# Gate projections of the first branch: from single blocks of 128 columns to pairs of blocks with seven half-size products

## The chip, the cores and the metric

The kernel runs on one core of a Trainium2 chip. The metric is the device time of one execution in microseconds (us). Five engines work side by side, each on its own queue in order: TensorE (PE, matrix products; its weight loads are shown as PEld), VectorE (DVE), ScalarE (ACT), GpSimd (POOL) and SyncE (SP, which here only issues DMAs). Sixteen DMA engines move data for all queues.

## The reference, cut to what matters

One encoder layer on 512 tokens of width 1024, in float32:

```
h = rmsnorm(x, pre_mix_w)
proj = h @ w_in                                   # q, k, v of two branches, and two gates
g_a, g_b = sigmoid(proj[..., gates] + b_gate)     # 1024 columns each
y_a = diff_attention(...)                         # branch A, 512 wide
y_b = neighbourhood_attention_2d(...)             # branch B, 512 wide
merged = g_a * (y_a @ w_branch_a) + g_b * (y_b @ w_branch_b)
x = x + rmsnorm(merged @ w_out, post_mix_w)
h = rmsnorm(x, pre_ffn_w)
f = (silu(h @ w_gate) * (h @ w_up)) @ w_down
x = x + rmsnorm(f, post_ffn_w)
```

The change concerns g_a (the gate of the first branch) and the merge.

## The kernel before

**Precision.** Each float32 operand is split into a high and a low part of a shorter type: the high part is a copy by ScalarE, the low part the difference, formed by VectorE. A product A x B is three matrix instructions into one bank: high x high, high x low, low x high (`mm3`, lines 217 to 219). Splitting a weight unit of 128 x 1024 takes one ACTIVATE (line 147) and one subtraction (line 153). Where VectorE is short of time, the low part is formed in another way: ScalarE writes minus the high part (line 73) and GpSimd issues a DMA that adds the raw values to it (line 74).

**Weights.** The class `Weights` holds all weight units in the order of their use. `load_to` issues their DMAs on SP into a pool of five raw buffers, `split_to` splits them in order, and each unit has a `place`: the pool for its two parts. `w` has four large buffers (`place_w`), `up` has 18 slots of 4 KB per partition for activations and temporaries, `up2` has 11 such slots and exists from the end of attention on. A slot of a pool is taken when the first instruction that writes the tile is placed.

**Stages.** After the norm, the transposed tokens lie in `hT`, as high and low parts, for the whole mixer. An interleaved list of steps (`main`, four steps per weight unit) runs the projections of both branches, with the stages of attention put between them by a table of positions (`events`). The last steps of `main` are the eight gate blocks of the second branch (`gate_b`, line 858: 24 matrix instructions of 512 columns, a sigmoid, and one product with what the second branch had given, kept in `pbt`). The last attention event falls into the fifth of these blocks. Then comes the loop that the change rewrites, lines 892 to 912, once for each of eight blocks of 128 gate columns:

```python
        W.split_to(UG["a", m] + 3)
        for k in range(KD):        # KD = 8: 24 matrix instructions of 512 columns
            mm3(bank, ...)
        nc.scalar.activation(sig, bank, AF.Sigmoid, bias=bg[:, m:m + 1])
        for k in range(4):         # branch A's projection: 12 of 512 columns
            mm3(bk2, ...)
        nc.vector.tensor_mul(sig, sig, bk2)
        nc.vector.tensor_add(sig, sig, pbt[m // 2][:, m % 2])
```

followed by the split of the merged block into a tile `mg`. The output projection (line 1005 on, weight units `UO`) needs all eight `mg`, for each block of 128 tokens in turn.

**The form with seven products.** The feed-forward stage already computes pairs of column blocks by a Winograd form of Strassen's scheme (line 1101 on). The 1024 x 256 weights of a pair are cut into quarters A11, A12, A21, A22 (512 rows by 128 columns, seen transposed), the tokens into quarters B11, B12, B21, B22 (512 features by 256 tokens). Weight sums S1 to S4 (`pair_steps`, line 64: six steps s0 to s5, run while the pair before is multiplied) and token sums T1 = B12 - B11, T2 = B22 - T1, T3 = B22 - B12, T4 = B21 - T2 (`t_sums`, made once) give seven products of 12 matrix instructions with 256 columns, instead of eight; small VectorE additions put the results together. The tables `ORDER` and `ORDER0` name the order of the products; the last of both is A22 x T4.

**What sets the order.** A planner lays out each engine's queue ahead of time from the program order and estimated durations: an instruction is taken early where its engine would stand idle and its operands and slot are there. In the start of the kernel (`manual_schedule`) the order is as written.

Of the kernel before, what the change touches and what calls it, by code (L numbers as in the profile page):

```python
# [14 lines left out]
S = 512  # L15
# [162 lines left out]
def block_kernel(ctx: ExitStack, tc: tile.TileContext, x, pre_mix_w, w_in,  # L178
# [71 lines left out]
    def add_branch(nm, w, j):  # L250
        n = w.shape[1]
        src = dram(w, 256 * j, [[n, 128], [128 * n, 4], [1, 256]])
        UBR[nm, j] = W.add(src, (4, 256), place_w)
# [11 lines left out]
    for m in range(8):  # L265
        UG["a", m] = W.add(cols128(w_in, 3072 + 128 * m), (8, 128), place_w)
        if m % 2 == 0:
            add_branch("a", w_branch_a, m // 2)
# [266 lines left out]
    def feat_slot(unit, evac, start=None):  # L535
        st = {}

        def step(q):
            def go():
                if q == 0:  # L540
                    st["bank"] = pmm.tile([128, 512], F32, tag="mm", name="mm")
                if q == 1:
                    W.split_to(unit + 4)
# [40 lines left out]
    def pb_slots(j):  # L584
        for s2 in range(2):
# [3 lines left out]
            def step(q, m=m, s2=s2, st=st):  # L589
                def go():  # L590
                    if q == 0:
                        st["bank"] = pmm.tile([128, 512], F32, tag="mm", name="mm")
                        if s2 == 0:
                            W.split_to(UBR["b", j] + 4)
# [271 lines left out]
    for m in range(8):  # L866
        gate_b(m)
    last_ev = max(events)
    assert last_ev < len(main), (last_ev, len(main))
    for n in range(len(main)):  # L870
# [3 lines left out]
        if n == last_ev:  # L874
            atk.close()
            stk_ps.close()
            up2 = ctx.enter_context(tc.tile_pool(name="u2", bufs=11))

# [4 lines left out]
    def wo_pl():  # L883
        wo_cnt[0] += 1
        if wo_cnt[0] <= 5:
            return place_pool(up2)()
        return (up2.tile([128, 1024], F32R, tag="u", name="whi"),
                up.tile([128, 1024], F32R, tag="u", name="wlo"))

    wo_place.fn = wo_pl  # L890
    mg = []
    for m in range(8):
        bank = pmm.tile([128, 512], F32, tag="mm", name="mm")
        bk2 = psB.tile([128, 512], F32, tag="b", name="b")
        if m == 4:
            W.raw_bufs = 3
        W.split_to(UG["a", m] + 3)
        hi, lo = W.get(UG["a", m])
        for k in range(KD):
            mm3(bank, hi[:, k], lo[:, k], hT[k // 4][:, k % 4, 0], hT[k // 4][:, k % 4, 1], k == 0, k == KD - 1)  # L900
        sig = U(F32, [128, 512], "sig")
        nc.scalar.activation(sig, bank, AF.Sigmoid, bias=bg[:, m:m + 1])
        hi, lo = W.get(UBR["a", m // 2])
        cs = slice(128 * (m % 2), 128 * (m % 2) + 128)
        for k in range(4):
            mm3(bk2, hi[:, k, cs], lo[:, k, cs], ya[k][:, 0], ya[k][:, 1], k == 0, k == 3)
        nc.vector.tensor_mul(sig, sig, bk2)
        nc.vector.tensor_add(sig, sig, pbt[m // 2][:, m % 2])
        t = U(F32R, [128, 2, 512], "mg")
        nc.scalar.activation(t[:, 0], sig, AF.Copy)  # L910
        nc.vector.tensor_sub(t[:, 1], sig, t[:, 0].bitcast(F32))
        mg.append(t)
# [173 lines left out]
    for m in range(2):  # L1086
# [4 lines left out]


    ORDER = (("A11", "B11", "A", "p"), ("S2", "T2", "B", "v"), ("S1", "T1", "C", "v5"),
             ("S3", "T3", "D", "c22"), ("S4", "B22", "C", "c12"), ("A12", "B21", "A", "c11"),
             ("A22", "T4", "D", "c21"))

    ORDER0 = (("A11", "B11", "A", "p"), ("A12", "B21", "F", "p11"), ("S4", "B22", "E", ""),
              ("S2", "T2", "B", "v"), ("S1", "T1", "C", "v5 p12"), ("S3", "T3", "D", "c22"),
              ("A22", "T4", "D", "c21"))
    gu = {}  # L1100
    for n, unit in enumerate(pairs):
# [4 lines left out]
        bank = {}  # L1106
        G = U(F32, [128, 2, 512], "G")
        pv = U(F32, [128, 3, 256], "pv")
        for i, (sn, tn, c, ev) in enumerate(ORDER if n else ORDER0):
            opens = c not in bank  # L1110
            if opens:
                bank[c] = psB.tile([128, 512], F32, tag="b", name="b")[:, :256]
            (sh, sl), (th, tl) = parts[sn], TQ[tn]
            kw = {} if opens else {"skip_group_check": True}
            for k in range(4):
                nc.tensor.matmul(bank[c], sh[:, k], th[:, k], start=opens and k == 0,  # L1116
                                 stop=False, **kw)
                nc.tensor.matmul(bank[c], sh[:, k], tl[:, k], start=False, stop=False, **kw)  # L1118
                nc.tensor.matmul(bank[c], sl[:, k], th[:, k], start=False, stop=k == 3, **kw)  # L1119
            for what in ev.split():  # L1120
                if what == "p":
                    nc.scalar.activation(pv[:, 0], bank["A"], AF.Copy)
                elif what == "v":
                    nc.vector.tensor_add(pv[:, 1], pv[:, 0], bank["B"])  # L1124
                elif what == "v5":
                    nc.vector.tensor_add(pv[:, 2], pv[:, 1], bank["C"])  # L1126
                elif what == "c22":
                    nc.vector.tensor_add(G[:, 1, 256:], pv[:, 2], bank["D"])
                elif what == "c12":
                    nc.vector.tensor_add(G[:, 0, 256:], pv[:, 1], bank["C"])  # L1130
                elif what == "p12":
                    nc.vector.tensor_add(G[:, 0, 256:], pv[:, 2], bank["E"])
# [138 lines left out]
```

## Time and profile before

| | |
|---|---|
| median of 3 runs | 747.43 us (747.38 to 747.66) |
| the profiled execution | 746.6 us, span 744.8 us |
| PE busy | 729.5 us, 98% of the span |
| PEld / DVE / ACT / POOL busy | 86% / 65% / 51% / 11% |
| granted TensorE clock, mean | 0.996 |
| DMA moved | 101.49 MB |

The span goes from the first to the last instruction; the profiled execution's own time has 1.8 us more around it. Durations of matrix instructions in the trace overlap (they are pipelined); what a product costs is read from the distance between starts.

### The profile page before, as it was taken

Reading aid. Unit: us, or ns where it says so; the run is one execution under the profiler, and the core shown is the slowest. Engines: PE = TensorE matmul, PEld = TensorE weight load, DVE = VectorE, ACT = ScalarE, POOL = GpSimd, SP = SyncE. Lnnn points to the kernel's source line nnn. Section 1 sums busy time; section 2 is a strip of 40 time slices with the busy share of each in tenths; the row PEclk is TensorE's granted clock in tenths of the full one; section 3 lists DMA queues with packets and bytes.
Section 4 is the critical chain, followed back from the end, with each engine's and each line's share of the span. In section 5 each row is a group of like instructions: output and inputs, shape, how many; then the busy total and the mean of one; then the engine's idle time right before and its main releaser. Section 6 shows DMA issues by size and latency. Waiting matters only on the chain. (4 is left out here: it accounts for less than half of the span.)

```text
span 744.8 us, 11240 instructions
## 1 busy us (share of the span) xinstructions
PE 729.5 (98%) x4368; PEld 643.5 (86%) x4368; DVE 481.8 (65%) x841; ACT 376.3 (51%) x611; POOL 83.0 (11%) x129
## 2 busy tenths in 40 slices
PE   8999999999999999999999999999999999999996
PEld 7887888877888888887889999999999998888884
DVE  6625788888776633466457987777778879222333
ACT  6413665665666722463124866666666656212211
POOL 1010001122330000000011111111111110000000
PEclk9999999999999999999999999999999999999999
DMA  9537645333311223263714588878878872443112
GB/s 257 173 87 210 169 107 163 100 99 99 99 58 30 85 74 96 91 220 114 197 49 148 122 179 198 198 181 195 188 173 186 215 192 103 142 169 118 51 45 68
DMA packets 102582, 101.49 MB, mean 136 GB/s; under 512 B 3537, under 2 KB 85473, under 8 KB 102530
## 3 DMA queue, kind: packets, MB, share of 16 engines
q1 hardware_dynamic: 96080, 82.82, 38.4%
q0 software_dynamic: 6448, 17.97, 12.0%
q8 instruction: 34, 0.56, 0.3%
q14 instruction: 18, 0.15, 0.1%
q10 hardware_dynamic: 2, 0.00, 0.0%
HBM read 74.56 MB, written 4.19 MB: 106 GB/s over the span
## 5 line engine op out<-in xcount | busy, mean ns | idle before, releaser
L153 DVE TENSOR_TENSOR w<-raw,w 128x1024 fp32r<-128x1024 f32 x67 | 82.0, 1226 | 83.7 <-ACT w L147 82.7
L147 ACT ACTIVATE w<-raw 128x1024 fp32r<-128x1024 f32 x67 | 70.4, 1053 | 61.8 <-PE b L219 51.8
L217 PE MATMUL mm<-hT,w 128*128 128x512 f32 x256 | 100.9, 394 | 0.3 <-DVE v L393 0.3
L218 PE MATMUL mm<-hT,w 128*128 128x512 f32 x256 | 99.9, 390 | 0.0
L219 PE MATMUL mm<-hT,w 128*128 128x512 f32 x256 | 99.8, 390 | 0.0
L1118 PE MATMUL b<-Tl,w 128*128 128x256 f32 x240 | 66.8, 278 | 0.0
L1116 PE MATMUL b<-Th,w 128*128 128x256 f32 x240 | 66.8, 278 | 0.0
L1119 PE MATMUL b<-Th,w 128*128 128x256 f32 x240 | 66.8, 278 | 0.0
L217 PEld LDWEIGHTS mm<-hT,w 128*128 128x128 f32 x256 | 48.1, 188 | 10.3 <-DVE v L393 0.7
L219 PEld LDWEIGHTS mm<-hT,w 128*128 128x128 f32 x256 | 48.1, 188 | 10.3
L218 PEld LDWEIGHTS mm<-hT,w 128*128 128x128 f32 x256 | 48.1, 188 | 9.2
L217 PE MATMUL b<-w,fh 128*128 128x512 f32 x144 | 56.0, 389 | 0.0
L218 PE MATMUL b<-w,fh 128*128 128x512 f32 x144 | 56.0, 389 | 0.0
L219 PE MATMUL b<-w,fl 128*128 128x512 f32 x144 | 56.0, 389 | 0.0
L74 POOL DMA_DIRECT2D w<-raw x40 | 34.5, 864 | 168.9 <-ACT w L73 131.1
L1119 PE MATMUL b<-Q,w 128*128 128x256 f32 x160 | 44.5, 278 | 0.9 <-DMA w<-raw 0.8
L1119 PEld LDWEIGHTS b<-Th,w 128*128 128x128 f32 x240 | 45.4, 189 | 0.0
L1116 PEld LDWEIGHTS b<-Th,w 128*128 128x128 f32 x240 | 45.3, 189 | 0.0
L1118 PEld LDWEIGHTS b<-Tl,w 128*128 128x128 f32 x240 | 45.3, 189 | 0.0
L1118 PE MATMUL b<-Q,w 128*128 128x256 f32 x160 | 44.3, 277 | 0.0
L1116 PE MATMUL b<-Q,w 128*128 128x256 f32 x160 | 44.3, 277 | 0.0
L982 ACT ACTIVATE junk<-b 128x512 f32<-128x512 f32 x16 | 9.6, 598 | 61.6 <-PE b L219 56.8
(231 smaller groups left out, 1883.0 us busy)
## 6 DMA issues: line engine op xcount, KB each, us to landing
raw<-in_w_in_dram SPq DMA_DIRECT2D x40, 512.0 KB, 4.2
raw<-in_w_gate_dram SPq DMA_DIRECT2D x22, 512.0 KB, 4.4
raw<-in_w_up_dram SPq DMA_DIRECT2D x22, 512.0 KB, 5.0
raw<-in_w_down_dram SPq DMA_DIRECT2D x22, 512.0 KB, 3.2
w<-raw POOLq DMA_DIRECT2D x20, 512.0 KB, 5.8
K<-K SPq DMA_DIRECT2D x24, 256.0 KB, 3.0
w<-raw POOLq DMA_DIRECT2D x20, 256.0 KB, 5.2
x<-in_x_dram SPq DMA_DIRECT2D x8, 512.0 KB, 8.9
```

Of the source, the lines that this page charges most:

```text
L74: nc.gpsimd.dma_start(lo, src, accum_op=ALU.add)
L147: self.nc.scalar.activation(hi, raw, AF.Copy)
L153: (engine or self.nc.vector).tensor_sub(lo, raw, hi.bitcast(F32))
L217: nc.tensor.matmul(bank, sh, mh, start=first, stop=False)
L218: nc.tensor.matmul(bank, sh, ml, start=False, stop=False)
L219: nc.tensor.matmul(bank, sl, mh, start=False, stop=last)
L982: nc.scalar.activation(junk, bs, AF.Square, scale=1.0 / 32.0, accum_out=ss[:, n:n + 1])
L1116: nc.tensor.matmul(bank[c], sh[:, k], th[:, k], start=opens and k == 0, stop=False, **kw)
L1118: nc.tensor.matmul(bank[c], sh[:, k], tl[:, k], start=False, stop=False, **kw)
L1119: nc.tensor.matmul(bank[c], sl[:, k], th[:, k], start=False, stop=k == 3, **kw)
```

## The change

The eight gate blocks of the first branch become four pairs in the seven-product form. `pair_products` is the feed-forward stage's loop body, made a function and called from both places. The token sums for it are made from `hT` by `ga_ahead`: for each quarter, ScalarE copies the high part and a DMA of GpSimd adds the low part (`block`); the four sums are formed by VectorE in place over the quarters, and split (`total`; T3 and T4 with the DMA form of the low part). These steps, and the first pair's weight steps, are taken two at a time behind the last eleven steps of `main`, after the last attention event. The pair's branch weight (256 columns) is split once per pair, into `up2`, and its two branch products and merges follow the pair's seven products. Three of the large weight buffers are held by a pair (parts A11/A12, S2/S1, S3/S4), and A22 lies in `up`. Output weight 0 goes to `w`, 1 to `up`, 2 to 5 to `up2`.

```diff
--- before.py
+++ after.py
@@ -247,10 +247,10 @@
 
     UBR = {}
 
-    def add_branch(nm, w, j):
+    def add_branch(nm, w, j, place=place_w):
         n = w.shape[1]
         src = dram(w, 256 * j, [[n, 128], [128 * n, 4], [1, 256]])
-        UBR[nm, j] = W.add(src, (4, 256), place_w)
+        UBR[nm, j] = W.add(src, (4, 256), place)
 
     order = ([("qk", "b", i) for i in range(4)] + [("qk", "a", 0), ("qk", "a", 1),
              ("qk", "a", 2), ("pb", 0), ("qk", "a", 3), ("pb", 1), ("pb", 2), ("pb", 3)])
@@ -262,10 +262,14 @@
     UG = {}
     for m in range(8):
         UG["b", m] = W.add(cols128(w_in, 4096 + 128 * m), (8, 128), place_w)
-    for m in range(8):
-        UG["a", m] = W.add(cols128(w_in, 3072 + 128 * m), (8, 128), place_w)
-        if m % 2 == 0:
-            add_branch("a", w_branch_a, m // 2)
+    ga_place = Late1()
+    br_place = Late()
+    UGP = []
+    for p in range(4):
+        UGP.append(W.add_pair([cols128(w_in, 3072 + 128 * m) for m in (2 * p, 2 * p + 1)],
+                              (8, 128), ga_place))
+        for j in {1: (0,), 2: (1,), 3: (2, 3)}.get(p, ()):
+            add_branch("a", w_branch_a, j, br_place)
     wo_place = Late()
     UO = {}
     for k in range(KD):
@@ -540,7 +544,7 @@
                 if q == 0:
                     st["bank"] = pmm.tile([128, 512], F32, tag="mm", name="mm")
                 if q == 1:
-                    W.split_to(unit + 4)
+                    W.split_to(min(unit + 4, UGP[0]))
                 hi, lo = W.get(unit)
                 for k in (2 * q, 2 * q + 1):
                     mm3(st["bank"], hi[:, k], lo[:, k], hT[k // 4][:, k % 4, 0], hT[k // 4][:, k % 4, 1],
@@ -591,7 +595,7 @@
                     if q == 0:
                         st["bank"] = pmm.tile([128, 512], F32, tag="mm", name="mm")
                         if s2 == 0:
-                            W.split_to(UBR["b", j] + 4)
+                            W.split_to(min(UBR["b", j] + 4, UGP[0]))
                     hi, lo = W.get(UBR["b", j])
                     for k in (2 * q, 2 * q + 1):
                         mm3(st["bank"], hi[:, k, 128 * s2:128 * s2 + 128],
@@ -865,6 +869,102 @@
 
     for m in range(8):
         gate_b(m)
+
+
+    ORDER = (("A11", "B11", "A", "p"), ("S2", "T2", "B", "v"), ("S1", "T1", "C", "v5"),
+             ("S3", "T3", "D", "c22"), ("S4", "B22", "C", "c12"), ("A12", "B21", "A", "c11"),
+             ("A22", "T4", "D", "c21"))
+
+    ORDER0 = (("A11", "B11", "A", "p"), ("A12", "B21", "F", "p11"), ("S4", "B22", "E", ""),
+              ("S2", "T2", "B", "v"), ("S1", "T1", "C", "v5 p12"), ("S3", "T3", "D", "c22"),
+              ("A22", "T4", "D", "c21"))
+    def pair_products(parts, TQ, nxt, first):
+
+        bank = {}
+        G = U(F32, [128, 2, 512], "G")
+        pv = U(F32, [128, 3, 256], "pv")
+        for i, (sn, tn, c, ev) in enumerate(ORDER0 if first else ORDER):
+            opens = c not in bank
+            if opens:
+                bank[c] = psB.tile([128, 512], F32, tag="b", name="b")[:, :256]
+            (sh, sl), (th, tl) = parts[sn], TQ[tn]
+            kw = {} if opens else {"skip_group_check": True}
+            for k in range(4):
+                nc.tensor.matmul(bank[c], sh[:, k], th[:, k], start=opens and k == 0,
+                                 stop=False, **kw)
+                nc.tensor.matmul(bank[c], sh[:, k], tl[:, k], start=False, stop=False, **kw)
+                nc.tensor.matmul(bank[c], sl[:, k], th[:, k], start=False, stop=k == 3, **kw)
...
+            if nxt and i in ((1, 2, 3, 5, 6) if first else (0, 1, 2, 4, 5)):
+                nxt.pop(0)()
+        return G
+
+
+    TA, TAr = {}, {}
+
+    def ga_pl(what):
+        if what == "a22":
+            t = U(F32R, [128, 2, 512], "w22")
+            return t[:, 0], t[:, 1]
+        return place_w(16, 1072)
+
+    ga_place.fn = ga_pl
+
+    def ga_steps(p):
+        return W.pair_steps(UGP[p], lambda: U(F32, [128, 1024], "S"), p == 0) if p < 4 else []
+
+    def ga_ahead():
+        def block(g, n):
+            def go():
+                r = TAr["B%d%d" % (g + 1, n + 1)] = U(F32, [128, 4, 256], "hq")
+                hi, lo = (hT[g][:, :, a, 256 * n:256 * n + 256] for a in range(2))
+                nc.scalar.activation(r, hi.bitcast(F32), AF.Copy)
+                nc.gpsimd.dma_start(r, lo.bitcast(F32), accum_op=ALU.add)
+                if (g, n) != (0, 1):
+                    TA["B%d%d" % (g + 1, n + 1)] = hi, lo
+            return go
+
+        def total(nm, a, b, over, by_dma):
+
+            def go():
+                r = TAr[over]
+                nc.vector.tensor_sub(r, TAr[a], TAr[b])
+                TAr[nm] = r
+                hi, lo = (U(F32R, [128, 4, 256], "Ta", up2) for _ in range(2))
+                nc.scalar.activation(hi, r, AF.Copy)
+                if by_dma:
+                    nc.scalar.activation(lo, hi.bitcast(F32), AF.Copy, scale=-1.0)
+                    nc.gpsimd.dma_start(lo, r, accum_op=ALU.add)
+                else:
+                    nc.vector.tensor_sub(lo, r, hi.bitcast(F32))
+                TA[nm] = hi, lo
+            return go
+
+        st = ga_steps(0)
+        return ([block(0, 0), block(0, 1), block(1, 1), st[0], block(1, 0),
+                 total("T1", "B12", "B11", "B11", False), total("T3", "B22", "B12", "B12", True)]
+                + st[1:5] + [total("T2", "B22", "T1", "B22", False), st[5],
+                             total("T4", "B21", "T2", "B21", True)])
+
+    ahead = []
     last_ev = max(events)
     assert last_ev < len(main), (last_ev, len(main))
     for n in range(len(main)):
@@ -875,6 +975,14 @@
             atk.close()
             stk_ps.close()
             up2 = ctx.enter_context(tc.tile_pool(name="u2", bufs=11))
+        if n > last_ev:
+            if n == last_ev + 1:
+                ahead = ga_ahead()
+            for _ in range(2):
+                if ahead:
+                    ahead.pop(0)()
+    for fn in ahead:
+        fn()
 
 
     psB = pstk.enter_context(tc.tile_pool(name="psB", bufs=6, space=PSUM))
@@ -882,34 +990,41 @@
 
     def wo_pl():
         wo_cnt[0] += 1
-        if wo_cnt[0] <= 5:
-            return place_pool(up2)()
-        return (up2.tile([128, 1024], F32R, tag="u", name="whi"),
-                up.tile([128, 1024], F32R, tag="u", name="wlo"))
-
+        if wo_cnt[0] == 1:
+            return place_w()
+        return place_pool(up if wo_cnt[0] == 2 else up2)()
+
+    br_place.fn = place_pool(up2)
     wo_place.fn = wo_pl
     mg = []
-    for m in range(8):
-        bank = pmm.tile([128, 512], F32, tag="mm", name="mm")
-        bk2 = psB.tile([128, 512], F32, tag="b", name="b")
-        if m == 4:
+    for p in range(4):
+        parts = W.parts.pop(UGP[p])
+        nxt = ga_steps(p + 1) + [lambda p=p: W.split_to(UBR["a", p] + 1)]
+        if p == 3:
             W.raw_bufs = 3
-        W.split_to(UG["a", m] + 3)
-        hi, lo = W.get(UG["a", m])
-        for k in range(KD):
-            mm3(bank, hi[:, k], lo[:, k], hT[k // 4][:, k % 4, 0], hT[k // 4][:, k % 4, 1], k == 0, k == KD - 1)
-        sig = U(F32, [128, 512], "sig")
-        nc.scalar.activation(sig, bank, AF.Sigmoid, bias=bg[:, m:m + 1])
-        hi, lo = W.get(UBR["a", m // 2])
-        cs = slice(128 * (m % 2), 128 * (m % 2) + 128)
-        for k in range(4):
-            mm3(bk2, hi[:, k, cs], lo[:, k, cs], ya[k][:, 0], ya[k][:, 1], k == 0, k == 3)
-        nc.vector.tensor_mul(sig, sig, bk2)
-        nc.vector.tensor_add(sig, sig, pbt[m // 2][:, m % 2])
-        t = U(F32R, [128, 2, 512], "mg")
-        nc.scalar.activation(t[:, 0], sig, AF.Copy)
-        nc.vector.tensor_sub(t[:, 1], sig, t[:, 0].bitcast(F32))
-        mg.append(t)
+            nxt += [lambda k=k: W.split_to(UO[k] + 1) for k in range(2)]
+        nxt.pop(0)()
+        G = pair_products(parts, TA, nxt, p == 0)
+        for fn in nxt:
+            fn()
+        for m in range(2 * p, 2 * p + 2):
+            sig = G[:, m % 2]
+            nc.scalar.activation(sig, sig, AF.Sigmoid, bias=bg[:, m:m + 1])
+        hi, lo = W.get(UBR["a", p])
+        for m in range(2 * p, 2 * p + 2):
+            bk2 = psB.tile([128, 512], F32, tag="b", name="b")
+            cs = slice(128 * (m % 2), 128 * (m % 2) + 128)
+            for k in range(4):
+                mm3(bk2, hi[:, k, cs], lo[:, k, cs], ya[k][:, 0], ya[k][:, 1], k == 0, k == 3)
+            sig = G[:, m % 2]
+            nc.vector.tensor_mul(sig, sig, bk2)
+            nc.vector.tensor_add(sig, sig, pbt[m // 2][:, m % 2])
+            t = U(F32R, [128, 2, 512], "mg")
+            nc.scalar.activation(t[:, 0], sig, AF.Copy)
+            nc.vector.tensor_sub(t[:, 1], sig, t[:, 0].bitcast(F32))
+            mg.append(t)
+        if p == 3:
+            W.split_to(UO[5] + 1)
 
 
     pstk.close()
...
@@ -1088,56 +1203,13 @@
     gu = {}
     for n, unit in enumerate(pairs):
         nxt = steps_of(n + 1)
         parts = W.parts.pop(unit)
         if nxt:
             nxt.pop(0)()
...
+        G = pair_products(parts, TQ, nxt, n == 0)
         gu[n % 2] = G
```

## Rows read from the trace of the kernel before

**Rows 1.** The page, parts 1 and 2: busy time, and the granted clock by slices.
```profile
PE 729.5 (98%) x4368; PEld 643.5 (86%) x4368; DVE 481.8 (65%) x841; ACT 376.3 (51%) x611; POOL 83.0 (11%) x129
...
PEclk9999999999999999999999999999999999999999
```

**Rows 2.** Windows: stretch, its length, busy us (instructions) per engine, clock, DMA share.
```profile
269.50:284.55 15.05, 15.05 (x68) 12.44 (x67) 6.10 (x7) 4.03 (x6) 0.00 (x0) 1.00 0.30 91
...
284.55:349.83 65.28, 65.28 (x289) 53.88 (x287) 34.11 (x39) 28.27 (x34) 0.00 (x0) 1.00 0.41 132
...
440.09:459.69 19.60, 19.60 (x173) 19.60 (x173) 15.33 (x23) 12.73 (x19) 3.49 (x5) 1.00 0.82 189
459.69:479.29 19.60, 19.53 (x170) 19.33 (x169) 15.66 (x24) 12.73 (x17) 3.45 (x5) 1.00 0.83 193
```

**Rows 3.** Waits of TensorE: us in total, times, longest.
```profile
PE warm L411 <- POOL mhalf L316: 1.5, 1, 1.5
PE o L708 <- DVE yb L719: 1.1, 1, 1.1
PE b L217 <- DVE sig L907: 1.0, 1, 1.0
...
PE b L1119 <- DMA w<-raw: 0.8, 1, 0.8
```

**Rows 4.** TensorE in order of time, the gate stage: start, us, instruction.
```profile
284.55 0.39 PE L217 MATMUL mm<-hT,w 128*128 128x512 f32 x1
...
289.99 0.39 PE L217 MATMUL b<-ya,w 128*128 128x512 f32 x1
...
347.11 0.39 PE L217 MATMUL b<-ya,w 128*128 128x512 f32 x1
...
350.95 0.47 PE L217 MATMUL b<-whi,mg 128*128 128x512 f32 x1 [0.96 <-DVE sig L907]
```

**Rows 5.** TensorE in order of time, two feed-forward pairs: first instructions of products.
```profile
451.43 0.28 PE L1116 MATMUL b<-Q,w 128*128 128x256 f32 x1
...
452.80 0.28 PE L1116 MATMUL b<-Th,w 128*128 128x256 f32 x1
...
459.60 0.28 PE L1116 MATMUL b<-Th,w 128*128 128x256 f32 x1
...
461.04 0.28 PE L1116 MATMUL b<-Q,w 128*128 128x256 f32 x1
...
471.03 0.28 PE L1116 MATMUL b<-Q,w 128*128 128x256 f32 x1
```

**Rows 6.** Groups by line, 245 to 351 us: busy us, mean ns of one.
```profile
L153 DVE TENSOR_TENSOR w<-raw,w 128x1024 fp32r<-128x1024 f32 x18 | 22.0, 1223 | 26.6 <-ACT w L147 26.6
L147 ACT ACTIVATE w<-raw 128x1024 fp32r<-128x1024 f32 x19 | 19.9, 1053 | 3.7 <-PE b L219 3.2 <-PE mm L219 0.5
...
L908 DVE TENSOR_TENSOR sig<-sig,pb 128x512 f32<-128x512 f32 x8 | 5.5, 691 | 0.2
...
L907 DVE TENSOR_TENSOR sig<-sig,b 128x512 f32<-128x512 f32 x8 | 5.4, 680 | 0.0
...
L911 DVE TENSOR_TENSOR mg<-sig,mg 128x512 fp32r<-128x512 f32 x7 | 4.8, 690 | 2.8 <-ACT mg L910 2.8
```

**Rows 7.** Groups by line, 440.09 to 479.29 us (four feed-forward pairs).
```profile
L76 DVE TENSOR_TENSOR Q<-S,Q 128x1024 fp32r<-128x1024 f32 x4 | 4.9, 1225 | 2.6 <-ACT Q L71 2.6
...
L71 ACT ACTIVATE w<-S 128x1024 fp32r<-128x1024 f32 x4 | 4.3, 1064 | 5.1 <-DVE S L96 5.1
...
L95 DVE TENSOR_TENSOR S<-raw 128x512 f32<-128x512 f32 x4 | 2.7, 686 | 0.0
...
L1128 DVE TENSOR_TENSOR G<-pv,b 128x256 f32<-128x256 f32 x4 | 1.7, 416 | 0.2
```

**Rows 8.** ScalarE in order of time: high half of the sixth output weight.
```profile
331.92 1.06 ACT L147 ACTIVATE whi<-raw 128x1024 fp32r<-128x1024 f32 x1 [3.19 <-DMA raw<-in_w_out_dram]
```

**Rows 9.** VectorE in order of time, 270 to 354 us.
```profile
270.32 0.75 DVE L837 SCALAR_TENSOR_TENSOR y<-o,sub,Rs 128x512 f32<-128x512 f32 x1
271.76 0.69 DVE L840 TENSOR_TENSOR ya<-y,ya 128x512 fp32r<-128x512 f32 x1 [0.70 <-ACT ya L839]
...
352.58 0.68 DVE L911 TENSOR_TENSOR mg<-sig,mg 128x512 fp32r<-128x512 f32 x1
353.19 1.22 DVE L153 TENSOR_TENSOR wlo<-raw,whi 128x1024 fp32r<-128x1024 f32 x1
```

**Rows 10.** DMA queues and issues, 440 to 482 us: MB, share; us to landing.
```profile
q0 software_dynamic: 1248, 3.54, 44.1%
...
w<-raw POOLq DMA_DIRECT2D x5, 512.0 KB, 5.6
```

**Rows 11.** The accumulating DMAs of line 74, whole run.
```profile
DMA to landing us min/median/max: 3.8/5.5/6.9
```

More of the change, by code (lines that the diff above doesn't have):

```diff
@@ L867, in block_kernel @@
         gate_b(m)
+    ORDER = (("A11", "B11", "A", "p"), ("S2", "T2", "B", "v"), ("S1", "T1", "C", "v5"),
[19 more added lines that the diff above has]
+                nc.tensor.matmul(bank[c], sl[:, k], th[:, k], start=False, stop=k == 3, **kw)
+            for what in ev.split():
+                if what == "p":
+                    nc.scalar.activation(pv[:, 0], bank["A"], AF.Copy)
+                elif what == "v":
+                    nc.vector.tensor_add(pv[:, 1], pv[:, 0], bank["B"])
+                elif what == "v5":
+                    nc.vector.tensor_add(pv[:, 2], pv[:, 1], bank["C"])
+                elif what == "c22":
+                    nc.vector.tensor_add(G[:, 1, 256:], pv[:, 2], bank["D"])
+                elif what == "c12":
+                    nc.vector.tensor_add(G[:, 0, 256:], pv[:, 1], bank["C"])
+                elif what == "p12":
+                    nc.vector.tensor_add(G[:, 0, 256:], pv[:, 2], bank["E"])
+                elif what == "c11":
+                    nc.scalar.activation(G[:, 0, :256], bank["A"], AF.Copy)
+                elif what == "p11":
+                    nc.vector.tensor_add(G[:, 0, :256], pv[:, 0], bank["F"])
+                else:
+                    nc.vector.tensor_add(G[:, 1, :256], pv[:, 1], bank["D"])
+            if nxt and i in ((1, 2, 3, 5, 6) if first else (0, 1, 2, 4, 5)):
+                nxt.pop(0)()
+        return G
@@ new lines, in block_kernel @@
+    TA, TAr = {}, {}
[27 more added lines that the diff above has]
+                    nc.gpsimd.dma_start(lo, r, accum_op=ALU.add)
+                else:
+                    nc.vector.tensor_sub(lo, r, hi.bitcast(F32))
[6 more added lines that the diff above has]
+                             total("T4", "B21", "T2", "B21", True)])
@@ L1089, in block_kernel @@
     ff_out(G, Uu)
[L1093 to L1099, printed above, removed]
     gu = {}
@@ L1105, in block_kernel @@
             nxt.pop(0)()
[L1106 to L1132, printed above, removed]
-                elif what == "c11":
-                    nc.scalar.activation(G[:, 0, :256], bank["A"], AF.Copy)
-                elif what == "p11":
-                    nc.vector.tensor_add(G[:, 0, :256], pv[:, 0], bank["F"])
-                else:
-                    nc.vector.tensor_add(G[:, 1, :256], pv[:, 1], bank["D"])
-            if nxt and i in ((0, 1, 2, 4, 5) if n else (1, 2, 3, 5, 6)):
-                nxt.pop(0)()
+        G = pair_products(parts, TQ, nxt, n == 0)
         gu[n % 2] = G
```

## The prediction

> **What bounds the kernel now.** I read the busy shares first: TensorE is busy 98% of the span and its granted clock stands at 9 tenths or more in every slice [rows 1]. Then the stages by windows: from 284.55 to 349.83, the stretch that the change rewrites, TensorE is busy 65.28 of 65.28 us and VectorE 34.11 [rows 2]. Then who kept TensorE waiting: over the whole run single waits of at most 1.5 us, none of them inside this stretch, and one of 1.0 us at its end, where the output projection waits for the last merge [rows 3]. So the stage ends when TensorE has streamed its columns. Fewer columns are time won, as long as the operands come in time.
>
> **Products removed and added.** A gate block of the first branch is 24 products of 512 columns. The first block starts at 284.55 and its branch products at 289.99, 5.44 us for 24, or 0.2267 us each; from that branch start to the eighth one at 347.11 there are seven periods of 8.16 us [rows 4]. A pair of gate blocks without its branch products costs 2 x 5.44 = 10.88 us. The new form is 7 half-size products of 12 instructions with 256 columns, 84 instead of 48 instructions. The feed-forward stage already runs this form, so its price can be read there: 451.43 to 452.80 is one product (1.37 us, 0.114 each), 459.60 to 461.04 is the slowest (1.44, 0.120 each), and a whole pair takes 461.04 - 451.43 = 9.61 us, the following one 471.03 - 461.04 = 9.99 [rows 5]. I take 9.61, because the other pair holds small waits that I cost separately. Gain: 4 x (10.88 - 9.61) = 5.08 us. The 24 branch products per pair stay as they are.
>
> **Weight preparation.** Eight single splits go (one copy on ScalarE, 1.05 us, and one subtraction on VectorE, 1.22 us, each [rows 6]). Per pair there come four half-width sums (0.69 us), two subtractions of 1.22 us, five small evacuations of 0.42, and on ScalarE copies of 1.06 us [rows 6, 7]. With the branch weight's split (1.22) and two merges of 0.68 + 0.69 + 0.69 [rows 6], VectorE has 2.7 + 2.4 + 2.1 + 1.2 + 4.1 = 12.6 us of work in a pair of 9.61 + 5.44 = 15.05 us, 84%. In the feed-forward stage VectorE had 15.33 us in 19.60, 78%, and TensorE stayed busy 19.60 and 19.53 us [rows 2]; there the pairs came faster. So I cost preparation at nothing where it lies beside products; if cover is short, the price is that of the feed-forward stage's slower pair, 9.99 - 9.61 = 0.38 us. Ends 0 and 4 x 0.38 = 1.5 us; I take 0.4, because the 5.44 us of branch products in every pair are slack that the feed-forward stage doesn't have.
>
> **Loads and slots.** The weight loads on SP keep their bytes and go in another order (both blocks of a pair, then its branch weight). A pair now holds three of the four large weight buffers, so the third of the next pair waits for the fifth product of this one; between that and its use lie two products and 5.44 us of branch products, against 1.06 + 1.22 us of work. Output weights 2 to 5 take the slots that the token sums leave; the last is free at the end of the seventh product of the last pair, 5.44 us before the output projection, and its split of 2.3 us fits. I take 0.2 us for the entry into that projection: the 1.0 us wait of [rows 3] stays, and at worst its releaser stands behind one more subtraction of 1.22. Ends 0 and 1.2.
>
> **Token sums, the new path into the first pair.** Four blocks (copy on ScalarE, then an accumulating DMA from GpSimd), four sums, their splits, and the first pair's own DMAs are issued while the last gates of the other branch run, before 284.55. That stretch has room: VectorE 6.10 and ScalarE 4.03 us of 15.05 [rows 2]. What can be late is the chain. The blocks take slots of a pool that is handed out in program order, as the trace shows: the low half of the sixth output weight was formed at 353.19, 20.2 us after its high half had ended (331.92 + 1.06), and right behind the last merge tile [rows 8, 9]. So the first block follows the last attention output (`y` at 270.32, `ya` until 272.45 [rows 9]); without the weight split ahead of it I put it at 271.0, and the third copy at 274.0. From there the accumulating DMAs set the pace. 3.54 MB of them took 44.1% of 42 us on the sixteen engines, 18.5 us, so one of 512 KB (0.524 MB) takes 2.74 us; from issue to landing it is 5.6 us, at least 3.8 [rows 10, 11]. If the third block (B22) is issued alone it lands at 274.0 + 3.8 = 277.8; if the first pair's own weight DMA (issued at about 270, landing 275.6) and two blocks stand ahead, at 275.6 + 3 x 2.74 = 283.8, and the fourth (B21) 2.74 later. After B22 come three sums of 1.23 one after another (T3, T2, T4), two ScalarE copies (2.1) and one more DMA (5.6): 11.4 us; after B21 it is 1.23 + 2.1 + 5.6 = 8.9. T4 is used in the seventh product, at 284.55 + 6 x 1.36 = 292.7. Early: T4 complete at 280.5 + 8.9 = 289.4, no stall. Late: 286.5 + 8.9 = 295.4, stall 2.7. I take the middle, 1.3, since both ends are equally far from what the rows decide.
>
> By the Trainium skill, "DMA: Bandwidth & Descriptors", section "Anatomy of one DMA — SWDGE (gpsimd) path", such a DMA takes about 2.0 us plus its bytes over 436e3 per us, for 512 KB an estimated 3.2 us. The trace's 5.6 us [rows 10] speaks against it while weight loads run beside it. With 3.2 the stall would be gone and the sum would be that of the second case below; I go by the rows.
>
> **Sum.** 5.08 - 1.3 - 0.4 - 0.2 = 3.2 us less. The profiled execution took 746.6 us; it becomes 743.4. The median of the runs shown, 747.43, is 0.8 above it, so the forecast is 747.43 - 3.2 = **744.2**. Own range of this case: gain 5.08 with nothing lost, 742.3, to all upper ends lost (2.7 + 1.5 + 1.2 = 5.4), 747.8.
>
> **Rivals.**
> *Nothing is late.* ScalarE is idle enough for the copies to go earlier and transfers don't queue: only 0.2 to 0.4 us lost, 742.4 to 742.7. For it: no wait of TensorE over 1.1 us in the feed-forward pairs' start, which prepares the same sums in a hurry; the longest is 0.8 us on such a DMA [rows 3]. Against: there the sums came without DMAs.
> *VectorE stands behind a landing.* It works its queue in order. If the first sum (T1, which needs the second block) is queued ahead of the weight sums and waits until B12 lands at 275.6 + 2 x 2.74 = 281.1, behind it stand four weight sums (2.7), T1's, S2/S1's and S3/S4's low parts (3.7), T3, T2, T2's low part and T4 (4.9): T4's sum ends at 292.4, its DMA lands at 292.4 + 2.1 + 5.6 = 300.1, and the seventh product stalls 7.4 us. 5.08 - 7.4 - 0.6 = -2.9: 750.3, slower. It decides from the end of T4's sum: up to 285.0 nothing is lost, at 289.5 the gain is used up, from 291 the kernel is measurably slower. For it: no row of before shows VectorE waiting for a DMA of GpSimd, so whoever laid the order out had no occasion to get it wrong or right. Against: 9 us of VectorE are free in that stretch [rows 2]. A milder form, the stall at 3 to 5.5 us, gives 746.0 to 748.5.
> *The half-size products don't reach 0.114 us here.* They read token halves and sums from other tiles than in the feed-forward stage, where the product whose two operands come from the small pool ran at 0.120 [rows 5]. If all 84 did, a pair takes 10.08, the gain is 3.2, and 747.43 - 3.2 + 1.9 = 746.1.
>
> **How the numbers follow.** This kernel's runs tell 0.2% (1.5 us) from no change: faster is under 745.9, slower over 748.9. Forecast 0.46 (faster but for 0.03); nothing late 0.20 (faster); mild stall 0.14 (0.02 faster, 0.12 same); slow products 0.07 (0.03 faster, 0.04 same); VectorE behind a landing 0.13 (0.12 slower, 0.01 same). Faster 0.43 + 0.20 + 0.02 + 0.03 = 0.68, same 0.03 + 0.12 + 0.04 + 0.01 = 0.20, slower 0.12. The range 742.0 to 748.3 leaves out the slow rival and a little at the low end. The likeliest case alone, and the two beside it that are faster, lie in 742.3 to 745.9.
>
> **What would show it.** After the change a pair should begin every 15.05 us from the second on, with 12 products in 1.36 to 1.44 us; TensorE's stretch from the first gate pair to the output projection should be 60 to 63 us instead of 66.4 (284.55 to 350.95 [rows 4]). TensorE's waits should name the DMA of GpSimd in the first pair, of 0 to 2.7 us. T4's sum on VectorE should end between 281 and 288. The forecast is wrong if waits of over 0.5 us recur in each pair (then preparation is the bound), if an earlier stretch grows (then the sums took slots or queue time from attention or the last gates), or if the output projection starts later than 351 minus the gain because its weights are late.

## The result: slower by 11 us, nearly all of it inside the rewritten stage

The changed kernel takes 757.98 us (median of 4 runs, 757.03 to 760.74) against 747.4 for the kernel before: a ratio of 1.0149, 95% interval 1.0137 to 1.016. The forecast was 744.2, its range ended at 748.3. The profiled execution took 758.2 us, span 756.3. (Single executions of 1,035 and 2,578 us among the runs of three experiments were disturbed; the medians below leave them out, so the first experiment stands at 744.96 here and at 745.25 in the expectations.)

First the page of after, which answers to [rows 1]: busy us and share, then the granted clock in 40 slices.

```profile
PE 732.8 (97%) x4512; PEld 652.4 (86%) x4512; DVE 505.0 (67%) x884; ACT 399.9 (53%) x644; POOL 96.8 (13%) x143
...
PEclk9999999999999998899999999999999999999999
```

TensorE's busy time rose by 3.3 us although there are fewer columns to stream, and two slices of the clock are low. The windows answer to [rows 2]: stretch, length, busy us (instructions) of PE, PEld, DVE, ACT, POOL, clock, DMA share, GB/s.

```profile
268.00:285.12 17.12, 17.12 (x82) 14.29 (x80) 6.35 (x9) 10.62 (x14) 7.09 (x6) 1.00 0.81 121
285.12:290.86 5.74, 2.91 (x26) 2.71 (x24) 5.05 (x6) 4.35 (x6) 0.46 (x1) 0.92 0.94 143
290.86:294.64 3.78, 3.09 (x13) 2.80 (x13) 3.78 (x5) 3.68 (x6) 0.39 (x1) 0.50 0.91 141
294.64:299.79 5.15, 5.15 (x38) 5.15 (x37) 5.12 (x9) 5.12 (x6) 1.71 (x2) 0.79 1.06 265
...
318.42:324.83 6.41, 6.41 (x31) 6.37 (x32) 3.78 (x6) 3.89 (x6) 0.00 (x0) 0.56 0.25 82
...
330.07:345.29 15.22, 15.22 (x109) 14.24 (x108) 12.92 (x20) 8.20 (x12) 0.86 (x1) 1.00 0.60 163
```

Up to 285.12 only 0.57 us is lost (the stage began at 284.55 before), and from 330.07 on a pair takes 15.22 us, close to the forecast of 15.05. The loss lies between. TensorE's waits in the stage (answering to [rows 3]: us in total, times, longest), and the stage's end (answering to [rows 4]):

```profile
PE b L893 <- ACT w L71: 2.8, 1, 2.8
PE b L893 <- ACT pv L899: 2.5, 1, 2.5
PE b L217 <- ACT mg L1023: 1.4, 1, 1.4
PE b L893 <- DVE pv L903: 1.3, 1, 1.3
PE b L895 <- DMA Ta<-hq: 0.8, 1, 0.8
PE b L896 <- DVE w L76: 0.7, 1, 0.7
```

```profile
290.86 0.58 PE L893 MATMUL b<-hT,w 128*128 128x256 f32 x1 [2.83 <-ACT w L71]
...
318.42 0.58 PE L893 MATMUL b<-hT,w 128*128 128x256 f32 x1 [1.34 <-DVE pv L903]
...
362.33 0.47 PE L217 MATMUL b<-w,mg 128*128 128x512 f32 x1 [1.42 <-ACT mg L1023]
```

The stage takes 362.33 - 285.12 = 77.2 us where the sum wanted 66.4 - 5.08 = 61.3. The first pair (285.12 to 307.96, less 5.44 for its branch products) took 17.4 us instead of 9.61, the second (307.96 to 324.60, which hold its seven products alone) 16.64; the third and fourth 9.75 and 10.0. So there are two losses, 7.8 and 7.0 us (the expectations below have 7.3 for the second, which takes in the first matrix instruction of its branch products). Idle time explains 2.83 + 0.69 + 0.83 of the first and 2.52 + 1.34 of the second. Most of the rest, 3.4 and 3.2 us, is the clock: from 290.86 to 296.77, and behind the second pair's second wait from 318.42 to 324.12, it stands at 0.50, the lower of its two levels. There the same instruction starts every 0.2135 us instead of 0.1133, which makes 2.5 and 2.8 us. What is left is 0.2 to 0.3 us of restart at each wait.

**The first loss.** VectorE of after in order of time (start, us, instruction, idle before it and its releaser); T1 is the first line 949:

```profile
276.98 0.68 DVE L96 TENSOR_TENSOR S<-S,raw 128x512 f32<-128x512 f32 x1
283.40 1.22 DVE L949 TENSOR_TENSOR hq<-hq 128x1024 f32<-128x1024 f32 x1 [5.74 <-DMA hq<-hT]
284.54 1.22 DVE L76 TENSOR_TENSOR w<-S,w 128x1024 fp32r<-128x1024 f32 x1
286.45 1.23 DVE L949 TENSOR_TENSOR hq<-hq 128x1024 f32<-128x1024 f32 x1 [0.69 <-DMA hq<-hT]
287.60 1.22 DVE L957 TENSOR_TENSOR Ta<-hq,Ta 128x1024 fp32r<-128x1024 f32 x1
288.73 0.68 DVE L107 TENSOR_TENSOR S<-raw,S 128x512 f32<-128x512 f32 x1
...
293.34 1.22 DVE L949 TENSOR_TENSOR hq<-hq 128x1024 f32<-128x1024 f32 x1
```

VectorE stands 5.74 us before T1 on a quarter's landing. Behind T1 in its queue is the last weight sum (line 107, 288.73), which ran at 281.07 in the first experiment below; its copy on ScalarE is what TensorE waited for at 290.86. T4's sum (293.34) ends at 294.56, its DMA lands at 304.0. The four accumulating DMAs, and their queue between 268 and 300 us (packets, MB, share):

```profile
L940 POOL DMA_DIRECT2D hq<-hT x4: 1317/1728/2046, 272.9 to 276.4; - x4
...
DMA to landing us min/median/max: 7.0/10.5/13.5
```

```profile
q0 software_dynamic: 2633, 3.77, 76.7%
```

76.7% of 32 us for 3.77 MB is 3.4 us of packet time per 512 KB, the figure that the expectations use. It is a little high, since packets overlap: from 280 to 287 us, when the trace shows nothing but these quarters in flight, 1.20 MB moved, which is 3.1 us per 512 KB. Four of them were issued within 5.2 us, behind a weight's DMA of the same size (issued at 271.45), so they came faster than they were carried: the last lands 13.5 us after its issue.

**The second loss.** ScalarE of after, and SP's load of the second pair's branch weight:

```profile
306.98 1.06 ACT L147 ACTIVATE whi<-raw 128x1024 fp32r<-128x1024 f32 x1 [5.41 <-DMA raw<-in_w_branch_a_dram]
...
308.90 0.70 ACT L1012 ACTIVATE G<-G,bg 128x512 f32<-128x512 f32 x1
...
315.15 0.63 ACT L1023 ACTIVATE mg<-G 128x512 fp32r<-128x512 f32 x1 [3.22 <-DVE G L1021]
315.69 0.36 ACT L899 ACTIVATE pv<-b 128x256 f32<-128x256 f32 x1
```

```profile
301.66 0.37 SPq L135 DMA_DIRECT2D raw<-in_w_branch_a_dram  x1
```

The planner had put the copy of the next branch weight ahead of the first pair's sigmoid. ScalarE stood 5.41 us for that load; the sigmoids, merges and `mg` copies came after it, and behind those the evacuation (line 899) without which TensorE could not go on at 316.10.

### The profile page after: what moved, and what is told of

Same layout as the page of the kernel before. It is cut to its first block, busy times and chain, and to the rows that moved or that the text cites. A ratio compares the mean times of both kernels' runs of the same rounds, so it can differ in the third digit from the quotient of the medians.

```text
span 756.3 us, 11674 instructions
## 1 busy us (share of the span) xinstructions
PE 732.8 (97%) x4512; PEld 652.4 (86%) x4512; DVE 505.0 (67%) x884; ACT 399.9 (53%) x644; POOL 96.8 (13%) x143
## 4 chain that ended last, share of the span: by engine, by line
PE 67%; DVE 13%; issue 6%; ACT 6%; DMA 5%; POOL 1%; DVEq 0%; POOLq 0%; ACTq 0%; SPq 0%
PE b L218 8%; PE b L219 8%; PE b L217 8%; PE b L893 7%; PE b L895 6%; PE b L896 6%; PE mm L401 5%; PE mm L217 4%; PE mm L218 4%; PE mm L219 4%; DMA w<-raw 2%; PE s L751 2%; DVE pl L702 2%; DMA hq<-hT 2%; DVE w L153 1%
## 5 line engine op out<-in xcount | busy, mean ns | idle before, releaser
L153 DVE TENSOR_TENSOR w<-raw,w 128x1024 fp32r<-128x1024 f32 x56 | 68.5, 1226 | 59.7 <-ACT w L147 58.6
L147 ACT ACTIVATE w<-raw 128x1024 fp32r<-128x1024 f32 x56 | 58.9, 1054 | 61.8 <-PE b L219 49.3
L217 PE MATMUL mm<-hT,w 128*128 128x512 f32 x192 | 76.0, 396 | 0.3 <-DVE v L397 0.3
L218 PE MATMUL mm<-hT,w 128*128 128x512 f32 x192 | 75.0, 391 | 0.0
L219 PE MATMUL mm<-hT,w 128*128 128x512 f32 x192 | 74.9, 390 | 0.0
L74 POOL DMA_DIRECT2D w<-raw x48 | 42.1, 876 | 216.4 <-ACT w L73 160.1
L71 ACT ACTIVATE w<-S 128x1024 fp32r<-128x1024 f32 x28 | 29.6, 1061 | 33.5 <-DVE S L96 29.4
L71 ACT ACTIVATE w<-raw 128x1024 fp32r<-128x1024 f32 (+1 forms) x48 | 40.0, 832 | 6.2 <-PE b L896 6.2
L219 PEld LDWEIGHTS mm<-hT,w 128*128 128x128 f32 x192 | 36.1, 188 | 7.8
L217 PEld LDWEIGHTS mm<-hT,w 128*128 128x128 f32 x192 | 36.1, 188 | 7.8 <-DVE v L397 0.7
```

Source lines behind the costliest of these rows:

```text
L71: nc.scalar.activation(hi, src, AF.Copy)
L74: nc.gpsimd.dma_start(lo, src, accum_op=ALU.add)
L147: self.nc.scalar.activation(hi, raw, AF.Copy)
L153: (engine or self.nc.vector).tensor_sub(lo, raw, hi.bitcast(F32))
L217: nc.tensor.matmul(bank, sh, mh, start=first, stop=False)
L218: nc.tensor.matmul(bank, sh, ml, start=False, stop=False)
```

## The experiments

Theory Q: the quarters' DMAs are late and VectorE's queue holds the rest behind them; the second loss follows from the first. W: the second loss is its own, ScalarE behind a weight load. P: the products themselves cost more here.

**Quarters by VectorE.** No copy, no DMA: one addition per quarter.

```diff
-                nc.scalar.activation(r, hi.bitcast(F32), AF.Copy)
-                nc.gpsimd.dma_start(r, lo.bitcast(F32), accum_op=ALU.add)
+                nc.vector.tensor_add(r, hi.bitcast(F32), lo.bitcast(F32))
```

> Edit: the four token quarters are formed by one addition of VectorE each (high + low part, 1.22 us), without ScalarE's copy and without the accumulating DMA of GpSimd; all else as in the changed kernel. Theory Q (the quarters' DMAs land late, VectorE holds everything else behind its first sum, and the loss in the second pair and the half clock follow from that): the first pair loses under 2 us instead of 7.8, the second under 1 us instead of 7.3, no stretch at half clock; 744 to 746 us. Theory W (the second pair's loss is its own: ScalarE stands behind the landing of the second branch weight, whenever the quarters come): the first pair is mended, the second still loses 5 to 7 us; 749 to 752 us. Theory P (half-size products cost more here than direct ones): no better than 755 us.

744.96 us, ratio 0.997 (0.9957 to 0.9982): 0.3% faster than the kernel before. Its stage takes 64.24 us, the clock is full throughout, and two waits are left (windows; TensorE's waits; ScalarE):

```profile
284.33:300.82 16.49, 15.40 (x109) 14.05 (x108) 13.90 (x21) 14.03 (x18) 3.45 (x4) 1.00 1.04 232
300.82:317.31 16.49, 16.49 (x122) 15.52 (x121) 12.94 (x20) 10.11 (x14) 1.74 (x2) 1.00 0.59 150
```

```profile
PE b L217 <- ACT mg L1022: 1.8, 1, 1.8
PE b L219 <- DVE wlo L153: 1.1, 1, 1.1
```

```profile
295.68 0.72 ACT L1011 ACTIVATE G<-G,bg 128x512 f32<-128x512 f32 x1 [0.34 <-DVE G L909]
...
297.53 1.06 ACT L147 ACTIVATE whi<-raw 128x1024 fp32r<-128x1024 f32 x1 [0.17 <-DMA raw<-in_w_branch_a_dram]
```

P falls: the products run at 0.113 to 0.115 us. The second loss is gone too, as Q says; but ScalarE's order is another one here (a sigmoid ahead of the weight's copy, and the load in time), so this run does not decide between Q and W.

**Each branch weight right behind its pair** (the list of units puts it there, and its split goes to the front of the pair's steps; quarters by DMA).

```diff
-        for j in {1: (0,), 2: (1,), 3: (2, 3)}.get(p, ()):
+        for j in (p,):
```

> Edit: in the order of the weights, each pair's branch weight comes right behind its own pair, so it is loaded and split before the next pair's weights; quarters by DMA as in the changed kernel. Theory Q: the first pair's 7.8 us stay; the second pair's 7.3 us shrink at most by half, because the merges of the first pair are late with it; 753 to 757 us. Theory W: the second pair's loss goes, 750 to 752 us. Theory P: 757 to 758 us, nothing changes.

752.95 us, 1.0073 (1.0047 to 1.0098). The first pair's waits stay (2.83, 0.69, 0.94), the second pair's are gone. The time lies between the two theories' figures, but the trace is clear: the second loss can be taken away alone, while the first stays whole.

**Both edits.**

> Edit: both of the edits before: quarters by VectorE, and each branch weight right behind its pair. Theory Q: as with the quarters alone or up to 1 us better, 743 to 745.5 us. Theory W: 743 to 745.5 us too, and at least 4 us better than the quarters alone. Theory P: no better than 753 us.

745.43 us, 0.9975 (0.9965 to 0.9986), no better than the first alone: where ScalarE doesn't stand on that load, its earlier place has nothing to give.

**Branch products ahead of the first pair's products**, as cover of 5.4 us (quarters by DMA).

> Edit: quarters by DMA as in the changed kernel, but the first pair's branch weight is split before all sums, and its 24 branch products (5.4 us of TensorE) stand before the pair's seven products instead of behind them. Theory Q: TensorE has work while the quarters land; the first pair loses 1 to 4 us instead of 7.8, and what follows from it shrinks too; 747 to 752 us. Theory W: the first pair gains the same, the second still loses 5 us or more; 752 to 755 us. Theory P: 755 us or more.

752.74 us, 1.0067 (1.0045 to 1.0089). That is 5.2 us off, but the cover isn't what gave most of it: the edit also puts every branch weight ahead of its own pair, and moving it behind its pair was worth 5.0 us by itself. In the trace the second pair's loss is gone, and the first pair with its branch products takes 306.04 - 285.43 = 20.61 us instead of 22.84, so the cover is worth about 2.2 us there. A wait of 2.63 us is left at 299.12, with a clock of 0.61 over the 3.9 us behind it.

**Low parts of T3 and T4 by VectorE** (`total(..., False)` for both; quarters by DMA).

> The kernel after, but the low parts of T3 and T4 are formed by VectorE instead of ScalarE and an accumulating DMA; the four quarters still come by DMA. Theory Q (the quarters' DMAs are late and VectorE's queue holds the first pair's weight sums behind the first token sum): the waits of 2.8 and 0.7 us at 290 to 293 stay, and with them a stretch of half clock, but T4 is whole about 8 us earlier (296 instead of 304), its wait of 0.8 us goes, the first merges are earlier and the second pair's waits of 2.5 and 1.3 us shrink to under 1 in all: 750 to 754. Rival L (T4's own landing is what costs: the waits at 290 are small change): 746 to 749. Rival that nothing of it matters as VectorE gets 2.4 us more work: 757 to 759.

754.9 us, 1.0105 (1.009 to 1.012). The time is just over theory Q's range. Waits of 2.53 and 2.41 stay in the first pair, with nothing at all in the second. T4's own landing is not the cause of the first loss; rival L falls. The second loss is gone although the branch weight is where the changed kernel has it; ScalarE's order, shown below the table, says why.

**Weight sums ahead of the token sums** in program order (`st[1:]` in front of the four `total`).

> The kernel after, but the steps of the first pair's weights are placed ahead of the four token sums; on VectorE's queue this takes the last weight sum and one low part out from behind T3 and T1's low part. DMAs, copies and work are the same. Theory Q: the wait of 2.8 us on ScalarE's copy of that weight sum falls below 1 us, the half clock behind it is shorter or gone, T4 lands as late as before (302 to 305): 752 to 756. Rival L (only the landing of T4 counts, the queue order is nothing): 757 to 758.5. If the order on VectorE were all of it: 746 to 748.

754.35 us, 1.0099 (1.0086 to 1.0113), within theory Q's range. The last weight sum ran at 285.45 instead of 288.73, and the 2.83 us wait became one of 1.57; new ones came on the copy and the low part of T2 (2.09, 0.68). VectorE still stood 5.74 us at T1 for the quarter. The order counts, and so does the landing.

**A contiguous source**: ScalarE first copies the low part into a tile of its own. Run twice, the second time for its profile.

```diff
+                c = U(F32, [128, 4, 256], "lq")
+                nc.scalar.activation(c, lo.bitcast(F32), AF.Copy)
                 nc.scalar.activation(r, hi.bitcast(F32), AF.Copy)
-                nc.gpsimd.dma_start(r, lo.bitcast(F32), accum_op=ALU.add)
+                nc.gpsimd.dma_start(r, c, accum_op=ALU.add)
```

> The kernel after, but ScalarE first copies each quarter's low part into a tile of its own, so that the accumulating DMA reads 4 KB in one piece per partition instead of four pieces of 1 KB; four more copies of 1.06 us on ScalarE. If the pieces make the landing slow (10.5 us, 3.4 us of sixteen engines each): issue on GpSimd falls from 1.3 to 2.0 us to about 0.9, landing to 5 to 7 us, and the time, in spite of 4.2 us more of ScalarE, to 748 to 755. If it is the queue (four DMAs and the weight's own behind one another): landing stays at 9 to 11 us, with 2.7 us of sixteen engines each, and the time is 756 to 760.

> The contiguous source once more, for its profile, since the profiled execution of the run before was disturbed. If the pieces of 1 KB make the landing slow: 5 to 7 us to landing, 0.9 us of issue, the sum T1 earlier than 281 (283.4 with pieces). If the queue does: 9 to 11 us to landing. Time as timed before: 752.8 to 754.4.

753.71 us, 1.0085 (1.007 to 1.0101); the second run is one execution, 750.5. The DMAs of the second run (issue ns, landing), and TensorE's longest wait:

```profile
L942 POOL DMA_DIRECT2D hq<-lq x4: 863/864/882, 273.3 to 279.6; - x4
...
DMA to landing us min/median/max: 5.0/6.5/6.9
```

```profile
PE b L893 <- ACT w L71: 2.9, 1, 2.9
```

Issue is 0.86 us and landing 6.5. Part of that is spacing: the extra copies spread the four issues over 7.1 us instead of 5.2. And still T1 waits (3.28 us) and the weight sum behind it is late: 2.9 us on TensorE. Even DMAs at nearly the 5.6 us that the prediction counted on didn't pay here, with VectorE's queue standing behind them.

**Two quarters by VectorE, two by DMA** (B11 and B12 added, so that T1 waits for none).

> The kernel after, but the two quarters that the first token sum needs (B11, B12) are formed by one VectorE addition each; B22 and B21 still come by ScalarE's copy and an accumulating DMA of 1 KB pieces. Theory Q with the queue (each of four such DMAs takes 3.4 us of the sixteen engines, so the last lands behind the three ahead of it): with two of them B22 lands within 8 us, the first sum waits for nothing, weight sums are not held, T4 is whole before 300, and the time is 745 to 748, near that of four additions (745.25). If a single such DMA is slow by itself (over 10 us however few there are): T3 stands in the first sum's place, waits of 1 to 3 us in the first pair stay, 750 to 755.

753.14 us, 1.0074 (1.0058 to 1.0089), not the 745 to 748 expected. The two DMAs land in 6.5 and 6.6 us although they read the same 1 KB pieces, so it was four of them in a queue that made them late. The first pair has waits of only 0.53 and 0.71 and loses 2.4 us (17.45 with its branch products, against 15.05), but the second loses 5.9 (20.94):

```profile
301.75 1.06 ACT L147 ACTIVATE whi<-raw 128x1024 fp32r<-128x1024 f32 x1 [4.21 <-DMA raw<-in_w_branch_a_dram]
...
303.66 0.71 ACT L1015 ACTIVATE G<-G,bg 128x512 f32<-128x512 f32 x1
```

```profile
PE b L893 <- ACT pv L899: 2.2, 1, 2.2
PE b L217 <- ACT mg L1026: 1.8, 1, 1.8
PE b L893 <- DVE pv L903: 1.5, 1, 1.5
```

This is the case that Q can't have: little of a first loss to carry on, and most of the second.

**Two by DMA and each branch weight earlier.**

> Both half measures at once: B11 and B12 by VectorE and B22, B21 by DMA (753.14 alone), and each branch weight loaded right behind its pair (752.95 alone). If there are two losses, each with a cause of its own (first pair: VectorE's queue behind the quarters' landings; second pair: ScalarE's copy of the next branch weight, queued ahead of the first pair's sigmoids, behind that weight's landing), each half measure took away one, and both together leave neither: 745 to 747. If the second pair's loss is only the first one carried on (theory Q as first put): the two half measures overlap, 750 to 753. If the two remaining accumulating DMAs cost by themselves: 748 to 750.

748.77 us, 1.0021 (1.0008 to 1.0033), over the 745 to 747 of two separate causes and within the 748 to 750 of remaining DMAs that cost by themselves: there is still a wait of 1.55 on T4, with 4.83 us at a clock of 0.65 behind it.

```profile
299.50:304.33 4.83, 4.83 (x19) 4.12 (x20) 2.31 (x4) 2.52 (x4) 0.86 (x1) 0.65 1.13 286
```

With the runs above it makes a table (us):

| quarters | branch weights in after's order | right behind their pair |
|---|---|---|
| four by DMA | 757.98 | 752.95 |
| two by DMA | 753.14 | 748.77 |
| by VectorE | 744.96 | 745.43 |

In the first two rows the weight's order is worth 5.0 and 4.4 us whether the quarters are four late DMAs or two: the second loss is not the first one carried on. Q is right about the first loss, and W about the second, but not "whenever the quarters come", as W was put. Three other traces keep the changed kernel's place of the weight (weight sums ahead, low parts by VectorE, the contiguous source's second run). They issue this load at 299.5 to 300.7 us, about as late as the changed kernel (301.66), and no wait of 1 us is left in their second pair, for in each ScalarE has one of the first pair's sigmoids ahead of the copy. So from the low parts' run:

```profile
303.94 0.71 ACT L1012 ACTIVATE G<-G,bg 128x512 f32<-128x512 f32 x1
304.55 1.05 ACT L147 ACTIVATE whi<-raw 128x1024 fp32r<-128x1024 f32 x1
```

The copy ahead of both sigmoids, and waiting, is found in the two traces with the loss (the changed kernel and two quarters by DMA) and in no other undisturbed one. With the quarters by VectorE a sigmoid stands ahead too, and the load lands in time; which of the two makes the weight's order worth nothing there was not separated.

**A lighter exit** on top of the first experiment: two raw buffers ahead instead of three in the last pair.

> Quarters by one VectorE addition each, as in the first run of that edit (745.25), and two raw weight buffers ahead instead of three in the last pair, which takes the first feed-forward weight's low part out from ahead of the last merges on VectorE. If the entry wait of 1.84 us comes from that low part (it stood behind ScalarE, which stood behind that weight's landing): the entry wait falls to about 0.9 and the time by 0.9, 744.2 to 744.6. If the weights of the output projection or of the feed-forward stage are late for it: 745.5 to 747.

752.23 us, 1.0066 (1.0053 to 1.008): a miss, and the second loss once more in another place. With fewer loads ahead the first feed-forward weight was issued at 343.78 instead of 338.82, and ScalarE's copy of it stands ahead of a merge's:

```profile
350.48 1.06 ACT L147 ACTIVATE w<-raw 128x1024 fp32r<-128x1024 f32 x1 [5.25 <-DMA raw<-in_w_gate_dram]
351.44 0.61 ACT L1022 ACTIVATE mg<-G 128x512 fp32r<-128x512 f32 x1
```

TensorE waited 5.41 us at the entry to the output projection, and then ran at a clock of 0.50.

**Quarters and low parts by VectorE**, no token DMA at all.

> Quarters by one VectorE addition each, and the low parts of T3 and T4 by VectorE too: no token sum waits for any DMA; VectorE has 2.4 us more work than with the additions alone, ScalarE 2.1 us less. If what is left of the loss (745.25 against the sum's 742.4) is T4's last DMA: 743.5 to 744.8. If it is the entry into the output projection (1.84 us) and the first branch weight (1.1 us), which stand: 744.8 to 746. If VectorE is full in the first pair: 746 to 748.

748.24 us, 1.0006 (0.9996 to 1.0015), over all three ranges. The waits in the first pair fell to one of 0.47, yet it is 3 us slower than the additions alone; the entry wait is 2.36. The profiled executions lie 3.9 us apart, of which the stage accounts for 0.6, the time ahead of it for 1.3 and the time behind it for 2.1; why, stays open. The best version found is the first experiment's.

## Why the prediction was wrong

- *Products.* Right. Undisturbed ones took 0.113 to 0.115 us, the one with both operands in the small pool 0.120; pairs three and four 9.75 and 10.0 us against 9.61. The first experiment's stage of 64.24 gained 2.2 us of the 5.08: it is 2.9 over the 61.3 of the sum, of which 1.1 is the first branch weight and 0.9 a longer entry wait. The rival of slow products is out. ("Nothing is late" comes to 742.6 to 742.8 by its own losses, not 742.4 to 742.7; nothing hangs on it.)
- *Token sums, the step that failed.* It put the stall at 1.3 us (0 to 2.7); the first pair lost 7.8. I let the DMAs queue on the sixteen engines at 2.74 us each; with 1 KB pieces they took 3.1, GpSimd issued them at 1.3 to 2.0 us each, and T1 began at 283.40. Worse, the step priced only the chain up to T4 and took VectorE's other work, the weight sums, as free to move past a landing; in its queue it was not. The rival "VectorE stands behind a landing" had the mechanism word for word and 0.13 of the chance; its price, a stall of 7.4 us, is near the 7.8 measured, which is luck, for the sum is another one: 4.35 of waits and 3.4 of clock and restarts, which no rival had. The place differs too: the third product waited first, not the seventh, which waited 0.83. T4's sum ended at 294.56, past the rival's mark of 291 (its 292.4 left out T1's own 1.22). "Against: 9 us of VectorE are free" was no argument: the time that passes in front of T1 is free for nothing queued behind it.
- *Weight preparation at 0.4 us, 1.5 at most, the second failure.* The sum 12.6 of 15.05 us was VectorE's busy time; what counted was ScalarE's order. A copy that waits for a load stood ahead of sigmoids that the next pair needed: 7.0 us in the second pair's trace, 5.0 and 4.4 in run time by the table. No case of the prediction held this; added to the rival's 750.3, the 7.0 us make 757.3, near the 757.98 measured, but the rival's part of that is a coincidence.
- *Entry and loads.* 0.46 us more than before (0.2 taken, 1.2 the bound). Right.
- *The page cited.* By "DMA: Bandwidth & Descriptors" of the Trainium skill, section "Anatomy of one DMA — SWDGE (gpsimd) path", 3.2 us were estimated; the landings of 5.0 to 6.9 us for 4 KB pieces and 7.0 to 13.5 for four at once speak against it under this load, where they stand in a queue.

## What to carry to other kernels

In this kernel a late transfer cost what stood behind its first reader in that engine's queue, not only what needed the data: so before pricing an added wait, write down the queue of the waiting engine and ask of each entry who waits for it. Busy shares say nothing about this. Work that can be done from on-chip data by an engine with room beat a copy and an accumulating DMA on the critical chain here (four additions of 1.22 us), although that engine, VectorE, is the busier one over the whole run (65% against ScalarE's 51% before).

## What the runs showed of the hardware

- The waits of TensorE in these two pairs cost about 1.8 times their length, (7.8 + 7.0) / (4.35 + 3.86): after 2.83 us of idling the clock stood at 0.50, the lower level, from 290.86 to 296.77, through the next wait of 0.69, and then rose. Not each wait does it: after 1.09 and 1.84 us in the first experiment it stayed at 1.00.
- Accumulating DMAs between on-chip tiles with 1 KB pieces took 1.3 to 2.0 us of GpSimd to issue, with 4 KB pieces 0.86. In stretches with nothing else in flight they moved 171 GB/s (1.20 MB in 280 to 287 us) with 1 KB pieces and 197 GB/s (1.09 MB in 279 to 284.5 us of the contiguous source's second run) with 4 KB pieces, or 3.1 and 2.7 us per 512 KB. The Trainium skill, "DMA: Bandwidth & Descriptors", section "Why small descriptors are slow (HBM only)", says that transfers between on-chip tiles don't suffer from small pieces; here, with accumulation, 1 KB pieces were 13% slower.
